# The even layer's gated and convolution projections in pairs of feature tiles by seven block products, with the context tiles beside the attention

## The chip, the cores and the metric

One core of a Trainium2 chip runs the whole program in one launch. The metric is device time in microseconds (us), the median over several executions. TensorE (PE) multiplies, VectorE (DVE), ScalarE (ACT) and GpSimd (POOL) do the rest, SyncE (SP) issues most of the DMAs.

## What is computed

A block of two layers on 1024 latent tokens (a grid of rows of 64) and 256 context tokens of width 1024, in float32. The even layer, cut to its core:

```
p = h @ w_in
q, k, v, g_a, a_f, a_b, c_b, c_c, c_x, g_b = _split_cols(p, EVEN_SIZES)
o_f, s_f = _gla_direction(q, k, v, log_gate(a_f, 0), s0_f)
o_b, s_b = _gla_direction(fl(q), fl(k), fl(v), fl(log_gate(a_b, 1)), s0_b)
o = _rmsnorm(o_f + fl(o_b), gla_g).reshape(bsz, length, GLA_V) * jax.nn.silu(g_a)
zc = _conv3_centered(c_c * c_x, conv_w)
y = c_b * zc * jax.nn.silu(g_b)
return jnp.concatenate([o, y], axis=-1), s_f, s_b
```

`_gla_direction` is a gated linear attention of 4 heads in chunks, forward and backward over the tokens. The odd layer is a recurrent unit in two directions. Each layer ends in an output projection, and the block in a norm.

## The kernel before

Features lie on the 128 partitions, tokens along the row. The normed input `h` of the even layer stays on chip as two float32r tensors, a high and a low part (`hhi`, `hlo`: 8 feature blocks by 1280 tokens). A product in float32 accuracy is three matmuls, `mm3`: high by high, high by low, low by high. A *unit* is one projection onto 128 features: `load_unit` loads its weights in two halves of 128x512 into the tiles `raw` (two buffers for the whole kernel) and `load_split` splits each by a ScalarE cast (line 111) and a VectorE subtraction (line 112) into a tile `hl` (six buffers). `proj` then multiplies it by the token chunks `CH`, 256 context tokens and twice 512 latents: 8 x 3 = 24 matmuls a chunk.

The gates of the attention (`emit_raw_gate`, units `w0f[8..15]`), and for each of eight feature tiles the convolution's four units (`emit_conv`: `cc`, `cx`, `cb` and its gate, `w0f[16..47]`) are 40 units in all. Their results go to DRAM (`gt_d`, `y0_d`). `presplit` splits the odd layer's weights in advance into DRAM (`w1s_d`), 20 halves a head, through the same `raw` and `hl` tiles.

The attention `emit_gla` runs a head at a time: three chunks backward, then three forward. A chunk is a gate (`pz`, a matmul, then ScalarE and VectorE in turn and a scan), factors (`qh`, `kh`, `k1`), transposes (`pk`), scores (`psc`), states (`pst`) and, forward, outputs (`po`), all in three PSUM banks of tag `G`, given out in program order. A scheduler orders each engine's instructions at build time: the program gives the priority, and what comes later fills in where what comes first is not ready. Behind head h the program has two gates, one convolution tile and 20 presplits, then q, k and v of the next head:

```
            for h in range(H):
                emit_gla(h)
                emit_raw_gate(w0f[8 + 2 * h], 2 * h)
                presplit(5)
...
                if h + 1 < H:
                    emit_qk(h + 1)
                    emit_v(h + 1)
    for ct in range(H, KD - 1):
        run(emit_conv(ct))
    run(emit_conv(KD - 1, CH[:2]))
```

Then come the remaining convolution tiles, under which the odd layer's modulation (`mod`, VectorE reductions `junk` of 128x1024 weights `wt`, line 586) runs, and the output projection (`out_group`), whose operands `ga` and `y` are loaded from `gt_d`, `oT_d` and `y0_d`. The last tile's last chunk is kept for between its groups (`rest`).

Of the kernel before, what the change touches and what calls it, by code (L numbers as in the profile page):

```python
# [28 lines left out]
H = 4  # L29
# [16 lines left out]
def hybrid_kernel(ctx: ExitStack, tc, xin, crow, frow, cols, consts, masks, w0f, w0va, w0v, wa2, wmT,  # L46
# [68 lines left out]
    def load_unit(src, name):  # L115
# [13 lines left out]
    hhi = hpool.tile([P, KD, T], F32R, name="hhi")  # L129
    hlo = hpool.tile([P, KD, T], F32R, name="hlo")  # L130

    def hk(k, c0, n):
        return hhi[:, k, c0:c0 + n], hlo[:, k, c0:c0 + n]

    def put_h(f, c0, n, ps, layer, sel, pool):

# [22 lines left out]

    w1s_d = dram.tile([5 * NB, P, 2, 512], F32, name="w1s_d")
    todo = [(b, j) for b in range(NB) for j in range(5)]

# [21 lines left out]
            ws += [(hi[:, k * P:(k + 1) * P], lo[:, k * P:(k + 1) * P]) for k in range(4)]  # L186
        return ws

    def emit_raw_gate(src, i, chunks=CH, tag="A"):
        for ps, c0, n in proj(load_unit(src, f"gt{i}_{chunks[0][0]}"), f"gt{i}", chunks, tag):  # L190
# [4 lines left out]
    def emit_conv(ct, chunks=CH, tag="A"):  # L195


        t0, t1 = chunks[0][0], chunks[-1][0] + chunks[-1][1]
        nm = f"{ct}_{t0}"
        z = vp.tile([P, T], F32, tag="z", name=f"z{nm}")  # L200
        zc = vp.tile([P, T], F32, tag="zc", name=f"zc{nm}")
        for ps, c0, n in proj(load_unit(w0f[16 + 4 * ct], f"cc{nm}"), f"cc{ct}", chunks, tag):
            S.copy(z[:, c0:c0 + n], ps)
        for ps, c0, n in proj(load_unit(w0f[17 + 4 * ct], f"cx{nm}"), f"cx{ct}", chunks, tag):
            V.tensor_tensor(z[:, c0:c0 + n], ps, z[:, c0:c0 + n], ALU.mult)
        V.tensor_scalar(zc[:, t0:t1], z[:, t0:t1], C("cw", 8 + ct), None, op0=ALU.mult)
        for lo_, hi_, w in ((t0, min(t1, NCTX), NCTX), (max(t0, NCTX), t1, 64)):
            if hi_ <= lo_:
                continue
            zr = z[:, lo_:hi_].rearrange("p (r i) -> p r i", i=w)  # L210
            cr = zc[:, lo_:hi_].rearrange("p (r i) -> p r i", i=w)
            V.scalar_tensor_tensor(cr[:, :, 1:w], zr[:, :, 0:w - 1], C("cw", ct), cr[:, :, 1:w],
                                   op0=ALU.mult, op1=ALU.add)
            V.scalar_tensor_tensor(cr[:, :, 0:w - 1], zr[:, :, 1:w], C("cw", 16 + ct), cr[:, :, 0:w - 1],
                                   op0=ALU.mult, op1=ALU.add)
        yield
        for ps, c0, n in proj(load_unit(w0f[18 + 4 * ct], f"cb{nm}"), f"cb{ct}", chunks, tag):
            V.tensor_tensor(zc[:, c0:c0 + n], ps, zc[:, c0:c0 + n], ALU.mult)  # L218
        SY.dma_start(y0_d[ct, :, t0:t1], zc[:, t0:t1])
        yield  # L220
        emit_raw_gate(w0f[19 + 4 * ct], 8 + ct, chunks, tag)

    def run(steps):
        for _ in steps:
            pass

    with sbuf("att") as ap:
# [124 lines left out]
        with sbuf("gla") as gp:  # L352
# [216 lines left out]
    for ct in range(H, KD - 1):  # L569
        run(emit_conv(ct))  # L570
    run(emit_conv(KD - 1, CH[:2]))

    rest = emit_conv(KD - 1, CH[2:], "B")


    with sbuf("mod") as mp:
# [36 lines left out]
        V.scalar_tensor_tensor(pl, pl, 2.0, mx, op0=ALU.mult, op1=ALU.add)  # L613
        V.tensor_scalar(rsc, pl, -8.0, None, op0=ALU.mult)
        V.tensor_scalar(rsh, pl, 4.0, None, op0=ALU.mult)

    def bcast_row(pool, ones, layer, s, name, tag):

# [447 lines left out]
```

## Time and profile before

| | |
|---|---|
| median of 3 runs | 1989.78 us (1987.29 to 1997.84) |
| profiled execution | 2002.68 us, span 2000.9 us |
| PE busy | 1932.0 us (97%) |
| DVE, ACT, POOL busy | 1317.8 us (66%), 961.3 us (48%), 105.2 us (5%) |
| DMA | 311.45 MB, mean 156 GB/s |
| attention, first gate of a head to that of the next | 174.7, 177.2 and 178.1 us |

A busy share is the time in which an engine has an instruction in work, over the span. Idle time of an engine counts only where another waits for it. Matmuls overlap in their pipeline, so a matmul's price is the distance between starts, not its duration.

### The profile page before, as it was taken

What the parts mean: (1) busy time and instruction counts of PE and PEld (TensorE: products, weight loads), DVE (VectorE), ACT (ScalarE), POOL (GpSimd) and SP (SyncE); (2) the same over time, 40 slices, a digit from 0 to 9 for tenths busy, and PEclk for the clock granted to TensorE, in tenths of its full rate; (3) what the DMA queues carried; (4) which work ended last, traced back from release to release, by engine and by line L of the source; (5) the groups of instructions that cost most, each with busy time, mean ns of one, the idle gap of its engine ahead of it and who ended that gap; (6) DMA issues with size and microseconds to landing.
All of it is one profiled execution on the core that took longest, in us unless ns stands there. A gap on an engine that the chain in (4) does not pass through costs nothing.

```text
span 2000.9 us, 27096 instructions
## 1 busy us (share of the span) xinstructions
PE 1932.0 (97%) x9884; PEld 1588.5 (79%) x9884; DVE 1317.8 (66%) x2103; ACT 961.3 (48%) x1690; POOL 105.2 (5%) x154
## 2 busy tenths in 40 slices
PE   9899999999999999999999899999999999998988
PEld 5777898888788888888776678878888888876767
DVE  6746436543552554388557474689999999996595
ACT  4333344334433433311345444267777776876452
POOL 1000000000000000000000000201111010100000
PEclk9999999999999999999999999999999999999999
DMA  9256217514721751366655665434333343324782
GB/s 357 82 195 199 78 50 252 175 43 146 244 89 33 245 192 53 124 223 197 205 175 178 209 222 173 139 111 127 120 118 120 115 121 121 116 81 156 264 290 88
DMA packets 162522, 311.45 MB, mean 156 GB/s; under 512 B 16338, under 2 KB 37202, under 8 KB 162260
## 3 DMA queue, kind: packets, MB, share of 16 engines
q1 hardware_dynamic: 140628, 267.78, 40.1%
q0 software_dynamic: 21760, 41.95, 7.5%
q8 instruction: 77, 1.26, 0.3%
q14 instruction: 57, 0.47, 0.1%
HBM read 221.05 MB, written 88.60 MB: 155 GB/s over the span
## 4 chain that ended last, share of the span: by engine, by line
PE 60%; DMA 19%; DVE 12%; ACT 5%; issue 4%; SPq 1%; POOL 0%; DVEq 0%; ACTq 0%; POOLq 0%
PE pjgt L126 4%; PE pjgt L127 4%; PE pjgt L125 4%; DMA rawpre<-in_w1f 4%; PE pjxr L125 4%; PE pjxr L127 4%; PE pjxr L126 4%; PE pO L126 3%; PE pO L125 3%; PE pO L127 3%; PE po L515 2%; DMA wt<-in_wmT 2%; DMA rawo<-in_w0out 2%; PE pv L125 2%; PE pv L126 2%
## 5 line engine op out<-in xcount | busy, mean ns | idle before, releaser
L125 PE MATMUL pjgt<-hhi,wgt 128*128 128x512 f32 (+1 forms) x640 | 240.6, 376 | 6.0 <-DVE zc L218 6.0
L125 PE MATMUL pO<-wo,yh 128*128 128x512 f32 x576 | 224.2, 405 | 17.6 <-ACT wo L111 16.6
L126 PE MATMUL pjgt<-hlo,wgt 128*128 128x512 f32 (+1 forms) x640 | 240.5, 376 | 0.0
L127 PE MATMUL pjgt<-hhi,wgt 128*128 128x512 f32 (+1 forms) x640 | 239.5, 376 | 0.0
L126 PE MATMUL pO<-wo,yh 128*128 128x512 f32 x576 | 231.1, 402 | 7.2 <-DVE wo L112 7.2
L127 PE MATMUL pO<-wo,yl 128*128 128x512 f32 x576 | 228.5, 399 | 0.0
L806 DVE SCALAR_TENSOR_TENSOR xc<-xp,col,xc 128x1283 f32<-128x1283 f32 (+2 forms) x102 | 149.8, 1476 | 3.2
L111 ACT CAST wo<-rawo 128x512 fp32r<-128x512 f32 x160 | 98.0, 619 | 110.7 <-DMA rawo<-in_w0out 74.9
L112 DVE TENSOR_TENSOR wo<-rawo,wo 128x512 fp32r<-128x512 f32 x160 | 108.5, 687 | 63.6 <-ACT wo L111 63.0
L125 PEld LDWEIGHTS pO<-wo,yh 128*128 128x128 f32 x576 | 109.3, 191 | 50.0 <-ACT wo L111 22.5
L125 PEld LDWEIGHTS pjgt<-hhi,wgt 128*128 128x128 f32 x640 | 121.0, 189 | 30.1 <-DVE zc L218 6.6
L126 PEld LDWEIGHTS pjgt<-hlo,wgt 128*128 128x128 f32 x640 | 121.1, 189 | 23.7 <-issue 1.1
L127 PEld LDWEIGHTS pjgt<-hhi,wgt 128*128 128x128 f32 x640 | 120.5, 189 | 23.4 <-issue 0.7
L126 PEld LDWEIGHTS pO<-wo,yh 128*128 128x128 f32 x576 | 109.7, 190 | 36.8 <-DVE wo L112 12.4
L125 PE MATMUL pjxr<-hhi,wxr 128*128 128x512 f32 (+1 forms) x384 | 137.4, 359 | 0.0
L126 PE MATMUL pjxr<-hlo,wxr 128*128 128x512 f32 (+1 forms) x384 | 137.1, 358 | 0.0
L127 PE MATMUL pjxr<-hhi,wxr 128*128 128x512 f32 (+1 forms) x384 | 136.8, 358 | 0.0
L127 PEld LDWEIGHTS pO<-wo,yl 128*128 128x128 f32 x576 | 109.8, 191 | 24.6 <-DVE yl L685 0.3
L112 DVE TENSOR_TENSOR wpre<-rawpre,wpre 128x512 fp32r<-128x512 f32 x80 | 55.1, 690 | 90.1 <-ACT wpre L111 89.7
L125 PE MATMUL pv<-wv,hhi 128*128 128x256 f32 (+1 forms) x320 | 91.8, 287 | 2.4 <-ACT v L387 2.4
L127 PE MATMUL pv<-wv,hlo 128*128 128x256 f32 (+1 forms) x320 | 92.9, 290 | 0.0
L126 PE MATMUL pv<-wv,hhi 128*128 128x256 f32 (+1 forms) x320 | 92.8, 290 | 0.0
(270 smaller groups left out, 4527.9 us busy)
## 6 DMA issues: line engine op xcount, KB each, us to landing
w1s_d<-wpre SPq DMA_DIRECT2D x160, 256.0 KB, 2.6
rawo<-in_w0out SPq DMA_DIRECT2D x96, 256.0 KB, 3.2
rawpre<-in_w1f SPq DMA_DIRECT2D x64, 256.0 KB, 3.1
wt<-in_wmT SPq DMA_DIRECT2D x32, 512.0 KB, 4.3
rawo<-in_w1out SPq DMA_DIRECT2D x64, 256.0 KB, 3.3
wxr<-w1s_d POOLq DMA_DIRECT2D x32, 512.0 KB, 3.8
wgt<-w1s_d POOLq DMA_DIRECT2D x32, 512.0 KB, 3.8
wm<-in_wmT SPq DMA_DIRECT2D x24, 512.0 KB, 8.1
```

What stands on the lines that cost most here:

```text
L111: S.copy(hi, raw)
L112: V.tensor_tensor(lo, raw, hi.bitcast(F32), ALU.subtract)
L125: PE.matmul(ps, a[0], b[0], start=first, stop=False)
L126: PE.matmul(ps, a[0], b[1], start=False, stop=False)
L127: PE.matmul(ps, a[1], b[0], start=False, stop=last)
L515: PE.matmul(ps[:, :DV], l, r, start=(i == 0), stop=(i == len(pairs) - 1))
L806: V.scalar_tensor_tensor(x, tap(j), cw[j], x, op0=ALU.mult, op1=ALU.add)
```

## The change

The latents' part of 36 units (eight gates, and the convolution's tiles without the last one, paired 0 with 4, 1 with 5, 2 with 6, and tile 3's four units in two pairs) moves behind the attention and is computed in 18 pairs. A pair of units times the latents is a 2x2 block product: two units by two halves of the input features, times two halves of the features by two halves of the tokens. It is done by seven block products instead of eight (Winograd's form of Strassen's): `pair` forms four combinations of raw weights on VectorE and splits them, `make_t` forms four combinations of `h` once and splits them into `T2`, `T3` and over parts of `hL` and `hC`, which are free by then (one quarter is put aside in DRAM, `b12_d`, and loaded back). Each product is 12 matmuls of 512 columns.

The context's part of the same units stays beside the attention, ten units of 256 tokens a head. Since `pair` needs three of each pair's four weight halves in split form, the context units also store theirs (`w0s_d`, two stores of 256 KB a half, 108 in all). `h` is now four tensors, high and low of the context (`hC`) and of the latents (`hL`). Of the last tile the context and first latent chunk stay as before.

```
--- before.py
+++ after.py
+            if i < len(save) and save[i] is not None:
+                for j, part in enumerate((hi, lo)):
+                    SY.dma_start(save[i][:, j], part.bitcast(F32))
...
             for h in range(H):
                 emit_gla(h)
-                emit_raw_gate(w0f[8 + 2 * h], 2 * h)
-                presplit(5)
-                emit_raw_gate(w0f[9 + 2 * h], 2 * h + 1)
-                presplit(5)
-                for _ in emit_conv(h):
+                for i in (2 * h, 2 * h + 1):
+                    emit_raw_gate(8 + i, i, CH[:1])
+                    presplit(5)
+                    run(emit_conv(i, CH[0]))
                     presplit(5)
...
+        for k in range(4):
...
+            b11, b12, b22, b21 = raw(k, 256), raw(k, 768), raw(4 + k, 768), raw(4 + k, 256)
+            V.tensor_tensor(b11, b12, b11, ALU.subtract)
+            V.tensor_tensor(b12, b22, b12, ALU.subtract)
+            V.tensor_tensor(b22, b22, b11, ALU.subtract)
+            V.tensor_tensor(b21, b21, b22, ALU.subtract)
+            for j, r, dst in ((1, b11, [t[:, k, 512:] for t in hL]), (2, b22, [t[:, k] for t in t23[0]]),
+                              (3, b12, [t[:, k] for t in t23[1]]), (4, b21, [t[:, k] for t in hv])):
+                S.copy(dst[0], r)
+                V.tensor_tensor(dst[1], r, dst[0].bitcast(F32), ALU.subtract)
...
+        x1, u2, u4, u5 = (tp.tile([P, 512], F32, tag=f"u{i}", bufs=1, name=f"u{i}{nm}") for i in range(4))
+        a11 = saved(0, 0)
+        r11, r21, r22, r12 = raw(0, 0), raw(1, 0), raw(1, 1), raw(0, 1)
+        p = product("A", a11, block(0, 256))
+        S.copy(x1, p)
+        V.tensor_tensor(r21, r11, r21, ALU.subtract)
+        V.tensor_tensor(r22, r22, r21, ALU.subtract)
+        s2 = parts(r22, "s2")
+        a12 = saved(0, 1)
+        p = product("A", s2, comb(2))
+        V.tensor_tensor(u2, p, x1, ALU.add)
+        V.tensor_tensor(r11, r22, r11, ALU.add)
+        s1 = parts(r11, "s1")
+        put(0, 0, product("G", a12, block(4, 256)), x1, x1)
+        s3 = parts(r21, "s3")
+        p5 = product("G", s1, comb(1))
+        V.tensor_tensor(u4, p5, u2, ALU.add)
+        a22 = saved(1, 1)
+        V.tensor_tensor(u2, product("A", s3, comb(3)), u2, ALU.add)
+        put(1, 1, p5, u2, u5)
+        V.tensor_tensor(r12, r12, r22, ALU.subtract)
+        s4 = parts(r12, "s4")
+        put(1, 0, product("A", a22, comb(4)), u2, u2)
+        put(0, 1, product("G", s4, block(4, 768)), u4, u4)
...
-    for ct in range(H, KD - 1):
-        run(emit_conv(ct))
-    run(emit_conv(KD - 1, CH[:2]))
...
+    T_ = make_t(tp)
+    for _ in emit_conv(KD - 1, CH[1]):
+        pass
...
+    for units, nm, put, around in jobs:
...
+        pair(tp, T_, units, nm, put)
...
+    for i in range(2):
+        G.dma_start(hL[i][:, 0:4, 512:], b12_d[i])
```

The built program of the change has 9089 rows of PE where the one before has 9305. Between the second and the third backward gate of head 1 (`pz1_1_768` and `pz1_1_256`), 45 matmuls of 256 and 62 of 512 columns of projections stand on PE before, and 60 of 256 in the change. SP's queue of the change, beside the attention of head 1 (`raw...` are loads of weights, `w0s_d` the new stores, `w1s_d` those of `presplit`):

```order
L189 DMA w1s_d_97<-wpre4_4_3456 128x512 x2
L97 DMA rawcc2_0_1_3470<-in_w0f 128x512
L122 DMA w0s_d_95<-wcc2_0_0_3465 128x512 x2
L97 DMA rawcx2_0_0_3503<-in_w0f 128x512
L122 DMA w0s_d_95<-wcc2_0_1_3472 128x512 x2
L97 DMA rawcx2_0_1_3510<-in_w0f 128x512
L122 DMA w0s_d_95<-wcx2_0_0_3505 128x512 x2
L97 DMA rawcb2_0_0_3546<-in_w0f 128x512
```

Before, the loads of a convolution unit had no store of their own weights between them; now each load stands behind the stores of the half before it.

VectorE of the change at the end of the attention (`rvo3_9` belongs to the last output of head 3, lines 599 to 610 are `make_t`, `junk0` and `modc` the modulation, `l_` small tiles of its end):

```order
L88 TENSOR_SCALAR rvo3_9_6555<-sso3_9_6553 128x1
L599 TENSOR_TENSOR b0_256_7111<-hL0_86,hL1_87 128x512
L599 TENSOR_TENSOR b0_768_7113<-hL0_86,hL1_87 128x512
L599 TENSOR_TENSOR b4_768_7115<-hL0_86,hL1_87 128x512
L599 TENSOR_TENSOR b4_256_7117<-hL0_86,hL1_87 128x512
...
L755 ISA junk0_9855,modc_9852<-wt0_9853,crb_9849 128x1024
L755 ISA modc_9852 128x1
L610 TENSOR_TENSOR T3_1_7108<-b0_768_7113,T3_0_7107 128x512
...
L665 TENSOR_TENSOR rga001_7355<-rga001_7355,rga011_7353 128x512
L630 TENSOR_TENSOR sga0s2_7373<-rga011_7353,sga0s2_7373 128x512
```

From the row behind `rvo3_9` to `sga0s2` are 113 rows; before, the reductions `junk` stood among the projections of tiles 4 to 7. PE of the change at the same place (`po3_9` and `pot3_9` are the last output and its transposes, `pga0` the first pair's products, the first by `hL`, the second by `T2` and `sga0s2`):

```order
L532 MATMUL po3_9_6548<-S0_3_8_6546,qf3_768_6435 128x256
L130 MATMUL pga0_7357<-hL0_86,aga000_7347 128x512
...
L130 MATMUL pga0_7357<-hL0_86,aga000_7347 128x512
L539 MATMUL pot3_9_6560<-ident_72,on3_9_6552 128x128 x2
L128 MATMUL pga0_7378<-T2_0_7105,sga0s2_7373 128x512
L129 MATMUL pga0_7378<-T2_1_7106,sga0s2_7373 128x512
```

Ten matmuls of the first product stand between the last output and the second product; before, twelve units of the tiles 4 to 6 and most of tile 7 stood behind the last head.

## Rows read from the trace of the kernel before

**Rows 1.** The page, parts 1 and 2: TensorE's busy time and granted clock.

```profile
PE 1932.0 (97%) x9884; PEld 1588.5 (79%) x9884; DVE 1317.8 (66%) x2103; ACT 961.3 (48%) x1690; POOL 105.2 (5%) x154
...
PEclk9999999999999999999999999999999999999999
```

**Rows 2.** Windows: length, then busy us (instructions) by engine, PEclk, DMA share, GB/s.

```profile
296.00:376.00 80.00, 79.69 (x436) 65.32 (x434) 48.82 (x100) 36.54 (x82) 0.00 (x0) 1.00 0.73 243
376.00:474.00 98.00, 96.83 (x609) 85.04 (x608) 35.93 (x84) 36.92 (x97) 5.47 (x10) 1.00 0.19 57
```

**Rows 3.** Timeline of PE, projections (start us, us): 24 starts of each width.

```profile
955.73 0.40 PE L125 MATMUL pjcx<-hhi,wcx 128*128 128x512 f32 x1
...
961.09 0.40 PE L127 MATMUL pjcx<-hhi,wcx 128*128 128x512 f32 x1
961.33 0.28 PE L125 MATMUL pjcb<-hhi,wcb 128*128 128x256 f32 x1
...
964.05 0.28 PE L127 MATMUL pjcb<-hhi,wcb 128*128 128x256 f32 x1
```

**Rows 4.** Timeline of PE: the first gate matmul of heads 1, 2 and 3.

```profile
298.00 0.38 PE L411 MATMUL pz<-aT,wst 64*128 64x256 f32 x1
...
475.21 0.38 PE L411 MATMUL pz<-aT,wst 64*128 64x256 f32 x1
...
653.26 0.38 PE L411 MATMUL pz<-aT,wst 64*128 64x256 f32 x1
```

**Rows 5.** Timeline of PE behind a wait ([idle before <-releaser]).

```profile
977.08 0.79 PE L125 MATMUL pjgt<-hhi,wgt 128*128 128x512 f32 x1 [4.32 <-DVE zc L218]
977.67 0.63 PE L126 MATMUL pjgt<-hlo,wgt 128*128 128x512 f32 x1
...
981.94 0.63 PE L127 MATMUL pjgt<-hhi,wgt 128*128 128x512 f32 x1
```

**Rows 6.** Timeline of ACT and DVE: first and last instruction of two chunks' factors.

```profile
298.41 0.47 ACT L414 ACTIVATE b<-pz,col 128x256 f32<-128x256 f32 x1
...
304.44 0.29 DVE L457 TENSOR_TENSOR k<-k,k 128x128 f32<-128x128 f32 x1
...
316.40 0.70 ACT L414 ACTIVATE b<-pz,col 128x512 f32<-128x512 f32 x1
...
326.50 0.42 DVE L458 TENSOR_TENSOR k<-kh,ends 128x256 f32<-128x256 f32 x1
```

**Rows 7.** Lines: count | busy us, mean ns of one | idle before, releaser.

```profile
L509 DVE SCALAR_TENSOR_TENSOR S<-S,dec,pst 128x256 f32<-128x256 f32 x64 | 30.6, 478 | 8.0 <-PE pst L504 5.9 <-DVE rvo L88 0.3 <-PE pz L411 0.3
...
L90 POOL TENSOR_TENSOR rro<-rvo,m 128x1 f32<-128x1 f32 x40 | 21.9, 548 | 741.9 <-DVE rvo L88 741.9
...
L519 ACT ACTIVATE on<-po,rro 128x256 f32<-128x256 f32 x40 | 18.9, 473 | 14.3 <-POOL rro L90 13.8
...
L466 ACT COPY k1T<-pk 128x512 f32<-128x512 f32 (+1 forms) x24 | 12.3, 511 | 17.3 <-PE pk L465 17.2
```

**Rows 8.** Windows of line 112 alone: length, DVE busy (instructions), PEclk, DMA.

```profile
296.00:376.00 80.00, 20.69 (x30) 1.00 0.73 243
```

**Rows 9.** Timeline of DVE: two instructions of 128x512 in a row.

```profile
324.02 0.68 DVE L459 TENSOR_TENSOR qh<-qh,q 128x512 f32<-128x512 f32 x1
324.63 0.68 DVE L456 TENSOR_TENSOR kh<-kh,k 128x512 f32<-128x512 f32 x1
```

**Rows 10.** Timeline of DVE: the modulation's reductions.

```profile
879.24 1.23 DVE L586 CUSTOM_DVE_ANT_0 junk<-wt,crb 128x1024 bf16<-128x1024 f32 x1 [1.90 <-DMA wt<-in_wmT]
...
880.50 1.23 DVE L586 CUSTOM_DVE_ANT_0 junk<-wt,crb 128x1024 bf16<-128x1024 f32 x1
```

**Rows 11.** Lines: SiLU and cast of the output projection's operands.

```profile
L668 ACT ACTIVATE ga<-ga 128x512 f32<-128x512 f32 (+1 forms) x80 | 46.9, 588 | 87.3 <-DMA ga<-gt_d 65.2 <-DMA ga<-g_d 20.4 <-DVE wo L112 1.4
...
L684 ACT CAST yh<-y 128x512 fp32r<-128x512 f32 (+1 forms) x80 | 45.8, 574 | 48.1 <-DVE y L681 21.8 <-PE pO L126 20.3 <-DVE y L679 5.7
```

**Rows 12.** DMA issues: count, KB each, median us to landing.

```profile
ga<-gt_d SPq DMA_DIRECT2D x32, 192.0 KB, 2.9
```

More of the change, by code (lines that the diff above doesn't have):

```diff
@@ L113, in load_split, with load_unit @@
         return hi, lo
-    def load_unit(src, name):
+    def load_unit(src, name, save=()):
         ws = []
@@ L193, in emit_raw_gate @@
             SY.dma_start(gt_d[i, :, c0:c0 + n], s[:, :n])
[L195 to L215, printed above, removed]
@@ new lines, in emit_conv @@
+    def emit_conv(ct, chunk, tag="A"):
+        c0, n = chunk
+        nm = f"{ct}_{c0}"
+        z = vp.tile([P, 512], F32, tag="z", name=f"z{nm}")[:, :n]
+        zc = vp.tile([P, 512], F32, tag="zc", name=f"zc{nm}")[:, :n]
+        for ps, _, _ in proj(load_unit(w0f[16 + 4 * ct], f"cc{nm}", kept(16 + 4 * ct, c0)), f"cc{ct}", [chunk], tag):
+            S.copy(z, ps)
+        for ps, _, _ in proj(load_unit(w0f[17 + 4 * ct], f"cx{nm}", kept(17 + 4 * ct, c0)), f"cx{ct}", [chunk], tag):
+            V.tensor_tensor(z, ps, z, ALU.mult)
+        short_conv(ct, zc, z, NCTX if c0 == 0 else 64)
@@ L568, in hybrid_kernel, with make_t, raw @@
                     emit_v(h + 1)
-    for ct in range(H, KD - 1):
-        run(emit_conv(ct))
-    run(emit_conv(KD - 1, CH[:2]))
-    rest = emit_conv(KD - 1, CH[2:], "B")
+    def make_t(tp):
+        t23 = [[tp.tile([P, 4, 512], F32R, name=f"T{j}_{i}") for i in range(2)] for j in (2, 3)]
+        for i in range(2):
+            SY.dma_start(b12_d[i], hL[i][:, 0:4, 512:].bitcast(F32))
+        hv = [t.rearrange("p (k a) n -> p k (a n)", a=2) for t in hC]
+        T = {}
+        for k in range(4):
+            def raw(kk, c0):
+                r = tp.tile([P, 512], F32, tag="r", bufs=4, name=f"b{kk}_{c0}")
+                hi, lo = hk(kk, c0, 512)
+                V.tensor_tensor(r, hi.bitcast(F32), lo.bitcast(F32), ALU.add)
+                return r
+            b11, b12, b22, b21 = raw(k, 256), raw(k, 768), raw(4 + k, 768), raw(4 + k, 256)
[7 more added lines that the diff above has]
+                V.tensor_tensor(dst[1], r, dst[0].bitcast(F32), ALU.subtract)
+                T[j, k] = tuple(dst)
+        return T
@@ new lines, in pair, with raw, saved, parts @@
+    def pair(tp, T, units, nm, put):
+        def raw(i, half):
+            r = tp.tile([P, 512], F32, tag="r", bufs=4, name=f"r{nm}{i}{half}")
+            load(r, w0f[units[i]][:, 512 * half:512 * half + 512])
+            return r
+        def saved(i, half):
+            hl = wpool.tile([P, 2, UW], F32R, tag="hl", bufs=6, name=f"a{nm}{i}{half}")[:, :, :512]
+            G.dma_start(hl, w0s_d[units[i], half])
+            return hl[:, 0], hl[:, 1]
+        def parts(r, name):
+            hl = wpool.tile([P, 2, UW], F32R, tag="hl", bufs=6, name=f"s{nm}{name}")
+            hi, lo = hl[:, 0, :512], hl[:, 1, :512]
+            S.copy(hi, r)
+            V.tensor_tensor(lo, r, hi.bitcast(F32), ALU.subtract)
+            return hi, lo
+        def product(tag, a, b):
+            ps = bank(tag, f"p{nm}")
+            for k in range(4):
+                mm3(ps, [t[:, k * P:(k + 1) * P] for t in a], b[k], k == 0, k == 3)
+            return ps
+        def block(k0, c0):
+            return [hk(k0 + k, c0, 512) for k in range(4)]
+        def comb(j):
+            return [T[j, k] for k in range(4)]
+        x1, u2, u4, u5 = (tp.tile([P, 512], F32, tag=f"u{i}", bufs=1, name=f"u{i}{nm}") for i in range(4))
[22 more added lines that the diff above has]
+        put(0, 1, product("G", s4, block(4, 768)), u4, u4)
@@ new lines, in hybrid_kernel, with start, conv @@
+    jobs = []
+    for i in range(0, 8, 2):
+        jobs.append(((8 + i, 9 + i), f"ga{i}", lambda r, *a, i=i: put_gate0(i + r, *a), None))
+    for ct in range(3):
+        c = (ct, ct + 4)
+        def start(c=c):
+            for i in c:
+                zt(zs, i)
+        def conv(c=c):
+            for i in c:
+                short_conv(i, zt(zcs, i), zs[i], 64)
+        fs = [lambda r, *a, c=c: put_z(c[r], *a), lambda r, *a, c=c: put_mul(zs[c[r]], *a),
+              lambda r, *a, c=c: put_y(c[r], *a), lambda r, *a, c=c: put_gate0(8 + c[r], *a)]
+        for j, nm in enumerate(("cc", "cx", "cb", "gb")):
+            o = 16 + j
+            jobs.append(((o + 4 * c[0], o + 4 * c[1]), f"{nm}{ct}", fs[j],
+                         (start, None) if j == 0 else (None, conv) if j == 1 else None))
@@ new lines, in hybrid_kernel @@
+    jobs.append(((28, 29), "cc3", put_ab, (lambda: zt(zs, 3), lambda: short_conv(3, zt(zcs, 3), zs[3], 64))))
+    jobs.append(((30, 31), "cb3", lambda r, *a: put_gate0(11, *a) if r else put_y(3, *a), None))
+    for units, nm, put, around in jobs:
+        before, after = around or (None, None)
+        if before:
+            before()
+        pair(tp, T_, units, nm, put)
+        if after:
+            after()
+    for i in range(2):
+        G.dma_start(hL[i][:, 0:4, 512:], b12_d[i])
+    rest = emit_conv(KD - 1, CH[2], "B")
@@ L615, in hybrid_kernel @@
         V.tensor_scalar(rsh, pl, 4.0, None, op0=ALU.mult)
+    tp_scope.close()
     def bcast_row(pool, ones, layer, s, name, tag):
```

60 lines of the change are left out of this document (51 added, 9 removed).

## Prediction

> **What bounds the kernel now.** I read the page first: TensorE (PE) is busy 97% of the span and the granted clock stands at its upper level in all slices [rows 1]. A mean hides stages, so the windows come next. In the attention two stretches alternate for each head. In the first, 296 to 376 us, PE is busy 79.69 of 80 us, VectorE 48.82, ScalarE 36.54 and the DMA engines 0.73; in the second the DMA share is 0.19 and PE is still full [rows 2]. The reader should see that nothing but PE is full there, and that PE is full because projections of the latents lie between the steps of the attention.
>
> The PE timeline gives the pace: in 24 matmuls of 512 columns the starts are (961.09 - 955.73)/23 = 0.233 us apart, in 24 of 256 columns (964.05 - 961.33)/23 = 0.118 us [rows 3]. The gate matmul that opens a head starts at 298.00, 475.21 and 653.26 us: 177.2 and 178.1 us a head, mean 177.6 [rows 4]. Six units of the cover (24 matmuls of 256 and 48 of 512 columns each, 14.0 us) take 84, the next head's q and k two units, 28, its v 240 matmuls of 256 columns, 28. So 37 us are the attention's own matmuls.
>
> **The change, part by part.** *Matmuls that go.* A pair of units on the latents took 2 x 2 x 24 = 96 matmuls of 512 columns; seven products of 12 are 84. Eighteen pairs save 216, at 0.233 us 50.3 us. The wait at 972 us, 4.32 us for `zc` and then 12 matmuls 0.427 apart ((981.94 - 977.67)/10) where 0.233 is the pace [rows 5], goes too, because that unit is no longer alone: 4.3 + 12 x 0.194 = 6.6 us.
>
> *The attention loses its cover.* The latents' halves of the 24 units that lay beside it move behind it; ten context units a head stay, 240 matmuls of 256 columns, 28 us. By the built order the PE work between a head's first gate and its last output is 37 + 28 + some 6 us of the next q: 72 us. How long does the attention need by itself? Gate, scan and factors of a chunk run from ScalarE's first instruction to VectorE's last: 298.41 to 304.73, 6.3 us for the context chunk, 316.40 to 326.92, 10.5 us for 512 columns, with weight splits among them [rows 6]. A head does this for three chunks in two directions: 2 x 27.3 = 55 us. The next chunk's gate can't be far ahead, since gate, scores, states and outputs take the three `G` banks in turn. Behind the factors a backward chunk has the transposes, their copy (0.51 us), a state matmul and two updates (0.48 each) before a bank is free: about 3 us. A forward chunk has the masks and, for every two tiles, a square, the power on GpSimd (0.55), the scaling (0.47) and a state update [rows 7]: about 5 us for the context chunk, 10 for the next and 15 with the last outputs. 55 + 9 + 30 gives 94 us, an estimate and the lower end.
>
> The upper end is the two `raw` buffers. From 296 to 376 us VectorE split 30 weight halves, one in 2.67 us [rows 8]. After the change 44 of them stand between the first gate and the last output of a head (20 of `presplit`, 20 of context units, 8 for the next head, less the four ahead of the gate), on the same in-order queues as the attention: 117 us. The new saves share SP's queue and the DMA engines: heads 0 and 1 move 126 and 122 transfers of 256 KB and some 2 MB of outputs, 35 and 34 MB, and at the 243 GB/s of that stretch [rows 2] 44/48 of it need about 130 us. I take 105 us, between 94 and 117, since both limits hold at once and neither alone. PE then waits 105 - 72 = 33 us in heads 0 to 2; in head 3, where the last unit's first latent chunk adds 83 matmuls of 512 columns, 105 - 85 = 20. Together +119 us (94: 75; 117: 167; with 130 in heads 0 and 1: 193).
>
> What do these waits do to the clock? After the one wait of 4.32 us the next matmuls ran at the lower level, 1.2 GHz, and lost 2.3 us [rows 5]. In the attention I charge nothing for that, since PE has slack there. The Trainium skill ("TensorE: Matmul & The Clock Gate", section "HAM oscillation — how this bites in real kernels") says that a kernel whose matmul groups are short beside the waits between them starts cold again in group after group, and the one restart in this trace agrees. By that rule PE would run the whole attention at half pace and the sum would be +310 us where mine is +128; it is the third rival below.
>
> *The combinations of the latents.* By the order `make_t` stands on VectorE behind the last `rvo3_9`, and PE has ten matmuls of the first product left then. The next product needs `s2`, 113 VectorE instructions on: 48 of `make_t` and 5 of the pair, each 128x512; 17 of the modulation's 1024-wide reductions, which before lay under projections; the rest tiny. At 0.61 us from start to start [rows 9] and 1.26 [rows 10], 53 x 0.61 + 17 x 1.26 + 26 x about 0.1 = 56 us, less 2 of PE's rest: 54 us of idle PE, and 2.3 us for the restart at the lower clock [rows 5]. Bounds 50 (some instructions overlap more) and 62 (the reductions wait for `wt`).
>
> *The first operands of the output projection.* SP's order has the loads `ga0_0_0` and `y0_0_0` behind the last pair's stores, so behind PE's last product: two vector instructions (0.61 each), a load of 2.9 us [rows 12], the SiLU (0.59), a multiply, the cast (0.57) [rows 11] and a subtraction, about 8 us, plus 2.3 for the restart: 10 us (4 to 16).
>
> *Costed at nothing.* In the pairs VectorE has 15 to 19 instructions of 128x512, 9 to 12 us, in 84 x 0.233 = 19.6 us of PE; two convolutions after `cx` fill one more pair nearly, and without that cover it would be 3 us in three places. A pair's 2.6 MB are 134 GB/s, below what rows 2 carry. The context matmuls were 256 wide before. The load that puts `hL` back has group 0 of the output projection above it.
>
> Sum: -50.3 - 6.6 + 119 + 56 + 10 = +128 us. The profiled run took 2002.68 us, 12.9 over the median of 1989.78 us; from the median, 2118 us.
>
> **The rivals.** *The attention stays covered*: its chain needs no more than PE's 72 us, so the 119 us vanish, and 1989.8 - 57 + 66 = 1999 us, 0.5% over; with hole and first operands at their lower ends (54) 1987, no change. For it: the scheduler put context units between all steps. Against: between two backward gates of head 1 stood 45 matmuls of 256 and 62 of 512 columns, 20 us, now 60 of 256, 7 us, where factors and states take 13. It decides from a chain of 72 us a head. To be faster by over 0.5% the hole would have to shrink as well, and VectorE's order excludes most of that.
>
> *The load ring binds by bytes*: about 130 us in the first two heads and more than 117 in the others, 2200 us and a little over. For it: 108 new stores of 256 KB. Against: the DMA share is 0.73 and not 1 where the ring ran before [rows 2], so the wait is partly latency, which more bytes don't lengthen.
>
> *Half clock through the attention*: 2 x 72 = 144 us in heads 0 to 2 and 170 in head 3, instead of 105, +182: 2300 us. For it: rows 5. Against: v and k run dense for some 45 us in each head, and PE's waits there should mostly be shorter than that one.
>
> **How the numbers follow.** The forecast, the sum with 94 to 130 us a head, 0.76: from -57 + 75 + 50 + 6 = +74 to -57 + 193 + 62 + 16 = +214, 2064 to 2204 us. Attention partly covered, 2000 to 2064 us, 0.08. Wholly covered, 1980 to 2000 us, 0.04; faster, 0.03. Above 2204 us, by bytes or by the clock, 0.09. The range 2055 to 2210 us holds about 8 in 10. About 0.5% (10 us) is what this kernel's runs can tell from no change: faster 0.03, same 0.04, slower 0.93.
>
> **What would show it.** Right: PE busy about 70% between a head's first gate and last output, gates of successive heads some 155 us apart, one PE gap near 54 us after the last `po`, and pairs 19.6 us apart. Wrong: PE full in the attention (then the chain is shorter than I add it up), a gap well under 50 us after it, or a pair that takes more than 22 us.

## The result, and the profile after

The changed kernel takes 2212.3 us in the median of 4 runs (2209.5 to 2215.8), the kernel before 1992.3 us on the same chip (1987.3 to 1997.8): 1.110 times as long, 95% interval 1.107 to 1.114. The forecast was 2118 us in a range up to 2210.

The page of the profiled execution (span 2210.8 us), TensorE's busy time and granted clock, as [rows 1]:

```profile
PE 1954.3 (88%) x9668; PEld 1593.8 (72%) x9668; DVE 1525.6 (69%) x2437; ACT 999.3 (45%) x1760; POOL 145.6 (7%) x210
...
PEclk9988987897897959999999999999999999999999
```

TensorE is busy for longer than before with 216 fewer matmuls, and no slice of 40 after the 15th shows a lowered clock (a digit under 9). So the first place to look is before 15/40 x 2211 = 829 us. Timeline of PE: the first gate matmul of each head, as [rows 4], the gates of the last two forward chunks of head 1, and the last output of heads 0, 1 and 3:

```profile
117.27 0.38 PE L428 MATMUL pz<-aT,wst 64*128 64x256 f32 x1 [1.01 <-DVE aT L415]
...
256.50 0.59 PE L532 MATMUL po<-S,qf 128*128 128x256 f32 x2
...
291.53 0.38 PE L428 MATMUL pz<-aT,wst 64*128 64x256 f32 x1
...
352.43 0.50 PE L428 MATMUL pz<-aT,wst 64*128 64x512 f32 x1
...
385.98 0.50 PE L428 MATMUL pz<-aT,wst 64*128 64x512 f32 x1
...
416.39 0.59 PE L532 MATMUL po<-S,qf 128*128 128x256 f32 x2
...
467.77 0.38 PE L428 MATMUL pz<-aT,wst 64*128 64x256 f32 x1
...
640.42 0.39 PE L428 MATMUL pz<-aT,wst 64*128 64x256 f32 x1
...
773.91 0.59 PE L532 MATMUL po<-S,qf 128*128 128x256 f32 x2
```

The heads come 174.3, 176.2 and 172.6 us apart. Before it was 177.6, with 288 matmuls of 512 columns more (67 us) and 96 of 256 fewer (11 us) in every head. These 56 us went behind the attention, and the heads came hardly closer; only head 3, behind which no further head stands, ended earlier (134 us behind its first gate instead of 180). Windows from gate to gate, then from the first gate to the end of the last output of heads 0, 1 and 3 (columns as in [rows 2]):

```profile
117.27:291.53 174.26, 134.59 (x819) 114.93 (x819) 86.37 (x189) 72.04 (x175) 5.48 (x10) 0.86 0.58 195
291.53:467.77 176.24, 140.93 (x844) 120.82 (x843) 86.68 (x190) 72.74 (x178) 5.65 (x10) 0.83 0.58 194
467.77:640.42 172.65, 134.89 (x844) 116.78 (x843) 85.63 (x190) 73.12 (x178) 5.47 (x10) 0.86 0.53 180
...
117.27:257.09 139.82, 100.15 (x549) 81.87 (x550) 83.50 (x184) 63.66 (x155) 4.93 (x9) 0.83 0.67 228
291.53:416.98 125.45, 90.14 (x492) 74.06 (x492) 81.73 (x182) 60.75 (x151) 5.10 (x9) 0.76 0.73 248
...
640.42:774.50 134.08, 102.13 (x554) 82.27 (x554) 86.44 (x190) 63.24 (x156) 5.80 (x10) 0.82 0.62 207
```

No engine is full there: TensorE waits 35 to 40 us a head and is stretched by a granted clock of 0.83 to 0.86 (part of the time at 1.2 GHz instead of 2.4), VectorE and the DMA engines have room. This points to a chain of steps that wait for each other. The longest wait of TensorE in head 1, then the longest of ACT (us in total, times, longest; first gate to last output):

```profile
PE psc L501 <- DVE kh L473: 17.4, 3, 6.5
...
ACT wpre L111 <- DMA rawpre<-in_w1f: 10.4, 11, 2.4
ACT k1T L483 <- PE pk L482: 7.4, 5, 3.2
ACT wcc L111 <- DMA rawcc<-in_w0f: 5.9, 4, 2.6
ACT wcb L111 <- DMA rawcb<-in_w0f: 5.9, 3, 2.8
ACT wpre L111 <- DMA rawpre<-in_w1ax: 4.9, 3, 3.5
```

TensorE waits most for `kh`, one of a chunk's factors: the attention's own chain. ACT, which works in that chain, waits for weights. Added up over all `raw` tiles of the head from gate to gate it is 41.4 us in which ACT stood before a cast whose weights had not landed. In the kernel before, the same sum is 34.8 us: the waits were there already, beside a TensorE that was full. One place where such a wait holds up a step of the attention is in ACT's timeline at the end of that head:

```profile
403.71 0.20 ACT L535 ACTIVATION_READ_ACCUMULATOR on<-po 128x1 f32 x1
406.95 0.62 ACT L111 CAST wq<-rawq 128x512 fp32r<-128x512 f32 x1 [3.05 <-DMA rawq<-in_w0f]
407.48 0.47 ACT L536 ACTIVATE on<-po,rro 128x256 f32<-128x256 f32 x1
```

The scaling of an output at 407.48 stands in order behind a cast of the next head's `wq`, and that waited 3.05 us for its load; the power that the scaling needs had been done at 404.8, and the transposes on TensorE wait for the scaling.

Behind the attention, timeline of PE at the combinations of the latents:

```profile
776.88 0.38 PE L539 MATMUL pot<-ident,on 128*128 128x128 f32 x2
831.80 0.80 PE L128 MATMUL pga<-T,sga0s 128*128 128x512 f32 x1 [54.53 <-ACT sga0s L629]
...
834.32 0.80 PE L128 MATMUL pga<-T,sga0s 128*128 128x512 f32 x1 [1.30 <-ACT sga0s L629]
...
839.60 0.59 PE L128 MATMUL pga<-hL,aga 128*128 128x512 f32 x1
```

A gap of 54.53 us, then a product of 12 matmuls in 7.8 us, 5.0 more than 12 x 0.233. A window of the pairs, and the start of the output projection on PE, whose last matmul of the pairs began at 1186.30:

```profile
860.00:880.00 20.00, 20.00 (x88) 16.09 (x87) 17.98 (x35) 2.97 (x5) 2.26 (x4) 1.00 0.93 284
```

```profile
1191.27 2.06 PE L797 MATMUL pggate<-dggate,ones 128*128 128x128 f32 x8 [4.57 <-DVE dggate L796]
1196.80 1.22 PE L797 MATMUL pggate<-dggate,ones 128*128 128x128 f32 x4 [3.47 <-DVE dggate L796]
1197.84 0.80 PE L128 MATMUL pO<-wo,yh 128*128 128x512 f32 x1
```

The pairs are dense at the upper clock level, though the DMA engines are busy 0.93 of the time in this window; the output projection loses some 10 us.

### The profile page after: what moved, and what is told of

It reads as the page before. It is cut to its first block, busy times and chain, and to the rows that moved or that the text cites. A ratio compares the mean times of both kernels' runs of the same rounds, so it can differ in the third digit from the quotient of the medians.

```text
span 2210.8 us, 27773 instructions
## 1 busy us (share of the span) xinstructions
PE 1954.3 (88%) x9668; PEld 1593.8 (72%) x9668; DVE 1525.6 (69%) x2437; ACT 999.3 (45%) x1760; POOL 145.6 (7%) x210
## 3 DMA queue, kind: packets, MB, share of 16 engines
q0 software_dynamic: 37504, 72.36, 11.3%
## 5 line engine op out<-in xcount | busy, mean ns | idle before, releaser
L130 PE MATMUL pjgt<-hL,wgt 128*128 128x512 f32 x272 | 107.7, 396 | 0.5 <-DVE wgt L112 0.5
L128 PE MATMUL pjgt<-hL,wgt 128*128 128x512 f32 x272 | 107.5, 395 | 0.0
L129 PE MATMUL pjgt<-hL,wgt 128*128 128x512 f32 x272 | 107.5, 395 | 0.0
L128 PE MATMUL pjxr<-hL,wxr 128*128 128x512 f32 x256 | 101.5, 397 | 0.0
L129 PE MATMUL pjxr<-hL,wxr 128*128 128x512 f32 x256 | 101.0, 396 | 0.0
L130 PE MATMUL pjxr<-hL,wxr 128*128 128x512 f32 x256 | 100.8, 395 | 0.0
L111 ACT CAST wpre<-rawpre 128x512 fp32r<-128x512 f32 x80 | 49.3, 616 | 68.1 <-DMA rawpre<-in_w1f 51.3
L839 ACT ACTIVATE ga<-ga 128x512 f32<-128x512 f32 (+1 forms) x80 | 46.9, 588 | 71.2 <-DMA ga<-gt_d 49.8
L1075 DVE TENSOR_TENSOR_SCAN a<-a,i 128x1024 f32<-128x1024 f32 x32 | 75.3, 2352 | 1.1
L129 PE MATMUL pv<-wv,hL 128*128 128x256 f32 (+1 forms) x256 | 72.9, 285 | 0.0
L130 PE MATMUL pv<-wv,hL 128*128 128x256 f32 (+1 forms) x256 | 72.6, 284 | 0.0
L128 PE MATMUL pv<-wv,hL 128*128 128x256 f32 (+1 forms) x256 | 72.6, 283 | 0.0
```

What stands on the lines that cost most here:

```text
L128: PE.matmul(ps, a[0], b[0], start=first, stop=False)
L839: silu = S.activation(ga, ga, AF.Silu)
L1075: V.tensor_tensor_scan(rv[3], rv[4], rv[5], rv[0][:, 255:256], op0=ALU.mult, op1=ALU.add)
```

## The experiments

Twelve kernels ran, eight of them beside single runs of the kernel before (1993.6 and 1994.5 us), four beside 7 runs (median 1994.9); all but e8 ran once, so differences under 10 us are not read. "Heads" are the distances of the first gate matmuls of heads 0 to 3; "attention" runs from the first of them to the end of head 3's last output; both were read from each run's timeline of PE.

```
kernel                          time     heads                 attention
before                          1992.3   174.7 177.2 178.1     709.7
the change                      2212.3   174.3 176.2 172.6     657.2
e1  no saves                    2187.3   170.8 169.9 164.5     638.4
e2  four raw                    2142.5   151.3 153.3 153.9     587.0
e3  presplit later              2187.8   138.4 132.4 138.0     530.7
e4  warm                        2224.0   174.7 178.1 173.9     666.6
e5  e1 + e3                     2184.1   132.4 139.2 136.6     525.3
e6  gates back                  2149.1   167.4 175.2 174.2     662.5
e7  direct products, no saves   2179.3   165.9 170.2 163.7     634.0
e8  hybrid                      2057.2   173.4 178.6 178.9     699.0
e9  reductions held             2198.7   172.0 176.0 174.6     656.8
e10 e1 + e2 + e9                2107.3   147.7 148.6 147.4     570.5
e11 warm, gates alone           2208.9   169.3 174.3 175.4     656.7
e12 presplit on GpSimd          2235.6   123.1 181.5 183.9     677.7
```

**Less load on the ring: e1, e2, e3.** The ring is the row of `raw` buffers through which weight halves come in; A is the time from a head's first gate to the end of its last output. The first edit is e1's (`saved` then loads and splits the half itself), the second e2's (`more_raw` is the attention's pool), the last two are e3's.

```diff
     def kept(u, c0):
-        if c0 or u >= 44:
...
+        return ()
...
+        if more_raw and next(raws) % 2:
+            raw = more_raw[0].tile([P, 512], F32, tag="raw", bufs=2, name=f"raw{name}")[:, :n]
...
                     emit_raw_gate(8 + i, i, CH[:1])
-                    presplit(5)
                     run(emit_conv(i, CH[0]))
-                    presplit(5)
...
         pair(tp, T_, units, nm, put)
+        presplit(5)
```

> The 108 stores of split weights are gone; the pairs load these halves whole and split them themselves (same arithmetic). A is the time from a head's first gate to its last output, 125, 131 and 133 us in heads 1 to 3 of the change. Theory 'load ring': the weight halves come one after another through SP's queue, where a load stands behind the stores of the half before it, and ACT and DVE wait in order for them; without the stores a half takes 2.67 us or less again, A falls to 117 us or below, and the time to about 2150 us (2130 to 2175). Theory 'clock': A is long because TensorE falls to 1.2 GHz again and again (granted 0.75 to 0.82 there); stores don't matter, A stays within 4 us and the time within 2195 to 2225. Theory 'chain': the attention's own steps need 125 us, the same 2195 to 2225.

> Four buffers for weight halves that come in instead of two, in the attention alone. Load ring, if it is the time from issue to landing that limits: A falls from 125 to 133 us to 110 or less, time 2110 to 2160 us. Load ring, if the bytes or the order of SP's queue limit: A within 5 us, time 2190 to 2220. Clock and chain: no change either, 2195 to 2225 us.

> The 80 weight halves that are split in advance for the second layer move from the attention to the pairs (five behind each of the first 16 pairs), so 24 of 44 halves a head stay beside the attention; TensorE's work there is unchanged. Load ring: A falls by about 20 x 1.5 to 20 x 2.7 us until the chain binds, to some 95 to 105 us, and the time by 4 x 25 to 4 x 35 to 2070 to 2115 us, if the pairs (19.6 us of TensorE each) take the splits for nothing. Clock or chain: A within 5 us and the time 2195 to 2225 us, more if the pairs are slowed.

e2 is the clear one: 2142.5 us, 70 less than the change, and its attention is 70.2 us shorter. Nothing but two more buffers for arriving halves was added; the program, its bytes and its stores stayed. Its ACT waits for `raw` tiles in head 1 are 8.7 us instead of 41.4. That A would fall to 110 didn't hold: A is 128 to 135 us. With the loads earlier the scheduler draws all of the next head's q and k and 58 to 78 of the 240 matmuls of its v in front of the last output, where the change has 36 to 118 of q and k and none of v. So A no longer measures heads 0 to 2, and the distance of the gates does: from a head's last output to the next gate it is 19 to 22 us instead of 34 to 51. In head 3, behind which no q, k or v stands, A fell by 5.6 us only (128.5). So most of the 70 us is work of the next head that now fills waits; no run separates that from loads which merely land earlier. Head 1 of e2, gate to gate, then heads 1 and 2 of e3 and A of its head 3:

```profile
269.94:423.23 153.29, 129.61 (x843) 114.10 (x843) 85.19 (x190) 72.59 (x179) 5.47 (x10) 0.91 0.64 223
```

```profile
258.06:390.44 132.38, 123.88 (x841) 108.44 (x840) 73.71 (x170) 61.70 (x157) 5.49 (x10) 1.00 0.42 138
390.44:528.44 138.00, 123.91 (x846) 109.89 (x845) 73.24 (x170) 62.39 (x159) 5.50 (x10) 0.98 0.34 112
...
528.44:650.37 121.93, 96.91 (x563) 79.22 (x562) 73.57 (x170) 53.62 (x136) 5.82 (x10) 0.90 0.30 101
```

With more bytes in the same time (223 against 194 GB/s) e2's head is shorter, so bytes didn't bind. In e3, with 24 halves a head instead of 44, TensorE is busy 124 of 132 to 138 us in heads 1 and 2 and stays near the upper level (granted 0.98 and 1.00): 8 to 14 us of waits are left where the next head's q, k and v fill in. In head 3, where they can't, 25 us of waits are left and A is still 121.9 us. e1 gave 25 us, two fifths of what its theory wanted, and ACT's waits for `raw` tiles in its head 1 are 41.9 us, no less than in the change: the new stores are a small part of it.

But e3's time fell by 24 us, though its attention is 126 us shorter. The other hundred went to the pairs, where the splits now stand. Waits of SP's queue in e3 from 740 to 1140 us:

```profile
SPq L189 <- ACT wpre L111: 78.5, 49, 4.8
SPq L189 <- DVE wpre L112: 54.2, 46, 4.6
...
PE pga L128 <- DMA aga<-w0s_d: 19.0, 3, 9.1
```

The stores of the splits wait for ACT and VectorE on SP's queue, and the loads behind them wait too. The last line is one of TensorE's own waits from 700 to 1140 us: 55 us in all for halves that were saved split (`aga<-w0s_d` and the like), and these are issued by GpSimd, not behind SP's stores, at a DMA share of 0.71 to 1.02 from 720 us on. So e3 alone doesn't tell order from bytes.

**Bytes or order in the pairs: e5.** The edits of e1 and e3 together.

> The stores of split weights are gone (pairs split all their halves themselves) and the 80 splits for the second layer stand behind the first 16 pairs. Where only the latter was moved, the heads came 132 to 138 us apart and the last output of head 3 ended 124 us earlier, but the pairs, at 6.4 MB each, took 24 us and more at a DMA share of 0.9 to 1.0 and gave 100 us back. Theory 'bytes in the pairs': at 1.8 MB for the pair and 3.8 MB for five splits, 5.6 MB in 19.6 us are 287 GB/s, below the 320 to 358 GB/s that those windows moved; the pairs take 20 to 21 us again and the time is 2075 to 2110 us. Theory 'order': the loads of the pair stand behind the splits' stores on SP's queue and VectorE has 24 to 27 instructions of 0.61 us a pair beside the reductions; the pairs stay at 23 us and more, time 2130 to 2190 us. In either case the heads stay 130 to 138 us apart (load ring); a clock or chain theory for the attention would have them return to 155 or more.

2184.1 us, in the range of the order theory. PE's waits from 700 to 1140 us, and one window:

```profile
PE pga L128 <- ACT sga0s L622: 52.2, 1, 52.2
PE pga L128 <- ACT waga L111: 27.3, 3, 10.6
PE pcc L128 <- ACT wacc L111: 23.8, 4, 9.5
...
800.00:820.00 20.00, 13.31 (x58) 10.37 (x56) 16.21 (x28) 3.10 (x5) 0.00 (x0) 0.89 0.98 363
```

From 820 to 1120 us the DMA share is 0.58 to 0.87 in its windows of 20 us with TensorE busy 15 to 20 of them, while the change itself ran its pairs dense at 0.93: there bytes don't bind. From 720 to 820 us the share is 0.93 to 0.98 with TensorE busy 9 to 19 of 20, and bytes aren't excluded. What binds behind 820 us is not separated either: e5 also moved the loads of the saved halves to SP's queue and gave ACT and VectorE their splits.

**The clock: e4, e11.** Both have the first edit, e4 alone the second; nothing of the computation is left out.

```diff
-                p3 = bank("G", f"psc{h}_{d}_{t0}").rearrange("p (t i) -> p t i", i=P)
+                p3 = bank("G", f"psc{h}_{d}_{t0}")
+                for _ in range(12):
+                    PE.matmul(p3, rmask[:, :P], rmask, start=True, stop=True)
+                p3 = p3.rearrange("p (t i) -> p t i", i=P)
...
                 ps = bank("G", f"pst{h}_{d}_{t}")
+                for _ in range(4):
+                    PE.matmul(ps[:, DV:], rmask[:, :P], rmask[:, :DV], start=True, stop=True)
```

> Extra matmuls whose results nobody reads are added to the attention (12 of 512 columns behind each gate matmul, 4 of 256 beside each state matmul, some 23 us a head at the upper clock level), in banks that are taken anyway. Clock: the granted clock between a head's first gate and last output rises from 0.75 to 0.82 to above 0.9, A falls by 10 to 20 us a head although TensorE does more, time 2130 to 2175 us. Load ring: the clock rises as well, but A stays within 4 us, 2200 to 2225. Chain with TensorE on it: A grows by up to 15 us a head, 2225 to 2275 us.

> Again matmuls whose results nobody reads, now only 12 of 512 columns behind each gate matmul (15 us a head), where the factors are computed and no step of the attention waits for TensorE, and none beside the state matmuls, where they stood in the chain. Clock: granted clock above 0.88 between a head's gate and last output and heads 160 to 168 us apart instead of 172.6 to 176, time 2165 to 2195 us. Load ring: the clock rises the same, the heads stay 172 to 178 us apart, time 2203 to 2222 us.

Windows of e11 from gate to gate:

```profile
116.88:286.14 169.26, 143.36 (x890) 118.30 (x891) 86.44 (x189) 70.95 (x175) 5.48 (x10) 0.92 0.59 200
286.14:460.46 174.32, 145.92 (x915) 120.08 (x915) 86.90 (x190) 72.58 (x178) 5.48 (x10) 0.93 0.58 197
460.46:635.87 175.41, 152.61 (x916) 126.43 (x915) 85.97 (x190) 72.95 (x178) 5.47 (x10) 0.88 0.53 177
```

The granted clock rises from 0.83 to 0.86 to 0.88 to 0.93 and the time stays (2208.9). In e4 the clock between a head's first gate and last output was 0.91 to 0.94 and the time 2224.0, 12 us more than the change; its second kind of matmul stands in the chain of the states, which may be why. A grew in two of three heads by more than the 4 us that the ring theory allowed. The theory that the clock lengthens the attention gets no support: the slow matmuls seem to lie where TensorE would wait. It isn't a clean test, since the added matmuls themselves take 16.8 us a head (72 x 0.233); e6 is the second one.

**Is TensorE's slack real: e6.**

```diff
-                    emit_raw_gate(8 + i, i, CH[:1])
+                    emit_raw_gate(8 + i, i)
...
-    for i in range(0, 8, 2):
-        jobs.append(((8 + i, 9 + i), f"ga{i}", lambda r, *a, i=i: put_gate0(i + r, *a), None))
```

> The eight gate units do their latents beside the attention again, by direct products (2 x 48 matmuls of 512 columns, 22.4 us of TensorE a head), and the four pairs of gate units are gone (4 x 19.6 = 78 us) with 12 of their stores. Load ring: the 174 us a head are set by the weight halves, of which there are as many as before, so the matmuls go into TensorE's 35 us of waits and the time that it runs at the lower clock: 172 to 180 us a head, time 2120 to 2150 us. If TensorE is itself on the path of the attention through its clock or its order: up to 22 us more a head, 2190 to 2225 us.

2149.1 us, 63 less: 78 us of pairs went, and 22 us of TensorE's work more in each head cost next to nothing (heads 167 to 175 us apart, the attention 5 us longer), at a granted clock of 0.93 to 0.94. By the theory that TensorE is on the path it would have been 2190 and more.

**The products themselves: e7.** `make_t` is gone and each pair does `proj` of its two units on `CH[1:]`, the rest as e1.

> The order of the change without its seven products: each pair's two units are done by direct products on the latents (96 matmuls of 512 columns), there are no combinations of the latents, and no stores of split weights. Beside the kernel with seven products and no stores (2187 us): +50 us for 216 matmuls at 0.233 us, -56 us for the stretch in which TensorE waits for the combinations, 2170 to 2190 us. If TensorE's wait behind the attention is mostly the reductions of the modulation, which stay, it would be +50 - 35 = 2195 to 2205 us.

2179.3 us against e1's 2187.3: without the products it is 8 us less, as the 50.3 us for 216 matmuls against the gap and its restart would have it. Two single runs tell no more than that the products gain nothing here.

**The gap behind the attention: e9.** The modulation's loads go by `load`, with `not_before[0]` set to the last load of the second pair.

> The modulation's loads stand behind those of the second pair, so its reductions leave the stretch in which TensorE waits for the combinations of the latents: by the built order 77 rows of VectorE instead of 113 stand between the last power of the attention and the second product's operand, none of them a reduction. By the prediction's sum for that stretch (53 x 0.61 + 17 x 1.26 + small ones) it falls from 54 to 32 to 35 us, time 2188 to 2198 us. If the loads of the first pair or the copies on ACT set it, it stays above 45 us and the time above 2203. If the reductions cost the pairs or the output projection as much later: the gap falls, the time doesn't.

Timeline of PE in e9, the first product that needs combinations:

```profile
815.74 0.80 PE L128 MATMUL pga<-T,sga0s 128*128 128x512 f32 x1 [38.78 <-ACT sga0s L629]
```

38.78 us instead of 54.53, and 2198.7 us, 13.6 less: both a little short of what was expected. The reductions were 16 us of the gap (17 x 1.26 = 21 were counted), and nearly all of that came off the time. The rest are `make_t`'s own instructions; one of them waited 3.22 us for a cast on ACT.

**Order or rate of the ring: e12.** Does a half cost because ACT and VectorE stand in order before it, or because each buffer is held for so long? `presplit`'s cast and subtraction are done by GpSimd.

```diff
-        S.copy(hi, raw)
-        V.tensor_tensor(lo, raw, hi.bitcast(F32), ALU.subtract)
+        (eng.tensor_copy if eng else S.copy)(hi, raw)
+        (eng or V).tensor_tensor(lo, raw, hi.bitcast(F32), ALU.subtract)
```

> The 80 splits for the second layer are done by GpSimd (cast and subtraction) instead of ACT and VectorE; loads, buffers, stores and SP's queue are those of the change. Load ring as a matter of rate (44 halves a head through two buffers, each held from its load to its split): GpSimd isn't faster than ACT and VectorE, so the heads stay 172 us apart or get longer, time 2205 to 2300 us. Load ring as a matter of order (ACT and VectorE wait in order for a half to land, and the attention's next step stands behind that): 20 of 44 halves no longer stop them, heads 150 to 165 us apart, time 2130 to 2180 us, less what GpSimd's own wait does to the power of each output that it computes.

2235.6 us. Lines of GpSimd from 290 to 466 us:

```profile
L112 POOL TENSOR_TENSOR wpre<-rawpre,wpre 128x512 fp32r<-128x512 f32 x20 | 27.2, 1363 | 0.9
L111 POOL CAST wpre<-rawpre 128x512 fp32r<-128x512 f32 x20 | 13.3, 665 | 115.4 <-PE pv L130 57.0 <-DVE wgt L112 31.4 <-DMA rawpre<-in_w1f 19.6
```

Taking 20 of 44 halves off ACT and VectorE bought nothing: 2235.6 us, the attention 20 us longer, heads 1 and 2 some 182 and 184 us long though ACT's waits for `raw` tiles fell to 29.9 and 23.2 us in them. That is in the range of the reading as a rate, but doesn't show it. GpSimd's subtraction takes 1363 ns (690 on VectorE), so it holds the buffer for longer; but GpSimd also stood 57.0 us in one wait for the next head's v (`pv` in the second line), the scheduler drew the next head's gate ahead (head 0 has 123 us), and GpSimd's power for each output stands behind its splits.

**Put together: e10 and e8.** e10 is e1, e2 and e9 in one.

> Four buffers for halves that come in, no stores of split weights, and the reductions held back, together. Singly the first two gave 70 and 25 us. Load ring: both act on the same wait, so together less than their sum, 75 to 95 us, and 15 to 20 us for the reductions: 2097 to 2122 us; heads 146 to 152 us apart. If they act on different waits, 95 us and more: 2080 to 2097. In either case slower than the kernel before by over 4%, since the attention without its cover has periods above 122 us and the combinations still stand open.

2107.3 us, 105 less than the change: 14 us as in e9 and 91 for e1 and e2 together, which is in the range for a shared wait but too near their sum of 95 to tell it from separate ones. It is the best form with all 18 pairs that ran, 5.7% over the kernel before.

e8 goes back to the cover of the kernel before and uses products behind it only: five pairs, tiles 4 and 5 and the last two units of tile 6, whose first two are done directly ahead of `make_t`.

```diff
-                    emit_raw_gate(8 + i, i, CH[:1])
...
+                emit_raw_gate(8 + 2 * h, 2 * h)
+                presplit(5)
...
+    for ct in range(H, KD):
+        run(emit_conv(ct, CH[:1]))
+    run(emit_conv(KD - 1, CH[1:2]))
...
     T_ = make_t(tp)
```

> The attention keeps the cover of the kernel before (gates and tiles 0 to 3 on all 1280 columns, no stores of split weights). Behind it stand direct units that don't need the combinations: tile 7's first latents and two units of tile 6, 39 us of TensorE beside some 40 us of VectorE for the combinations; then five pairs by seven products (tiles 4, 5 and half of 6); the modulation's reductions begin behind the second pair's loads. Load ring (so no loss where TensorE's cover is long): heads 175 to 178 us apart as before, no gap over 5 us behind the last output, 5 x 12 matmuls x 0.233 = 14 us less and the 6.6 us wait gone: 1965 to 1985 us. If the reductions delay the output projection, or the combinations still show as a gap: 1990 to 2020 us.

2057.2 us, 1.031 times the kernel before (1.029 to 1.033), above both of the ranges that were expected. The attention did as expected, 699 us against 710 before. What it lost stands behind that; PE's waits from 820 to 1070 us, and one of VectorE's from 960 to 1060 us:

```profile
PE pggate L807 <- DVE dggate L806: 34.7, 1, 34.7
PE pO L128 <- ACT yh L865: 15.6, 1, 15.6
PE pcc L128 <- ACT scc4s L634: 14.8, 1, 14.8
...
DVE junk L765 <- DMA wt<-in_wmT: 12.5, 9, 2.4
```

65 us. The combinations still stick out by 14.8 us, and the reductions that were held back (`junk`) arrive on VectorE at the start of the output projection, whose gate rows (`dggate`) stand behind them. VectorE is full from 920 to 980 us; at the end of the stretch the last reductions wait for their own loads. In e9, where 18 pairs stand above the output projection, TensorE waits 7.8 us for the gate rows. A version that spreads the reductions over the output projection's first group wasn't tried; none of the kernels that ran beats the kernel before.

## Why the prediction was wrong, point by point

*Direction and mechanisms.* Slower, by the attention without its cover and by the gap behind it: both hold. The sum came to +128 us; the measured change is +220.

*The step that failed* is the size of the attention's term: "I take 105 us, between 94 and 117, since both limits hold at once and neither alone." A was 139.8, 125.5, 131.3 and 134.1 us (start of the first gate to the end of the last output), above both ends. By the distance of the gates it is 174 instead of 155 us, 58 us in three heads, and 29 in head 3 (134 - 105), 87 in all. That alone would have made the forecast 2205. Both limits were set too low:

- The upper end, from the ring. 2.67 us a half was measured beside a TensorE that was full [rows 2, 8]. The trace has 42 to 45 halves in A, about as counted, but they came one in 2.92 to 3.18 us.
- The lower end, from the chain. In e3's head 3, with 20 halves fewer and no next head behind it, A is 121.9 us and TensorE waits 25 us, where 94 and 94 - 85 = 9 were counted (e5: 117.2 and 20). In head 1 of the change the last two forward chunks took 33.6 and 31.0 us from gate to gate and to the last output; 20.5 and 25.5 were added up. In heads 1 and 2 of e3 the waits are 8 to 14 us, fewer than the 22 counted, since work of the next head fills them, which the sum didn't have.

So a value between two limits had no support: A lay above both. e2 shows how much of it hangs on the ring. Two more buffers bring the heads to 151 to 154 us, near the 155 of the forecast, 65 us in all; of the 29 us of head 3 they take 6, and 20 halves fewer take 12 (17 in e5). What the rest of head 3 is stays open: a chain that was added up too short, or one that is slowed by what stands beside it.

*The rival "load ring by bytes"* came near in time (2200 and a little over) by a reason that doesn't hold: e2 moves the same bytes faster, and e1, with 27 stores a head less, gives 25 us. The argument against it in the prediction, that at a DMA share of 0.73 the wait is partly latency, was right, and should have been carried into the price.

*The clock* was charged nothing "since PE has slack there". By the profile alone that looks wrong: in A TensorE waited 35 to 40 us in heads 0 to 2, near the 33 of the forecast, and was busy 90 to 100 us instead of 72, at a granted clock of 0.76 to 0.83. But e11 raised the clock and e6 added 22 us of matmuls a head, and neither moved a head by more than 7 us, which bears the prediction out; that the clock costs exactly nothing isn't shown. The Trainium skill ("TensorE: Matmul & The Clock Gate", section "HAM oscillation — how this bites in real kernels") describes restarts at the lower clock in matmul group after matmul group. The trace agrees that the clock falls again and again there; the prediction's sum by that rule, +310 us, didn't come about, as the clock wasn't low throughout (that would be 0.50).

*The matmuls that go, the gap, the first operands.* 54.53 us against 54; the restart behind it cost 5.0 us (1.3 of it a further wait) against 2.3; the output projection began 11.3 us behind the last pair, 3.3 of it `pggate` matmuls, and some 2 us of restart, together about 10, against 10. Pairs dense, 88 matmuls in 20 us, against 19.6 us for 84. e7 fits the balance of 50 against 56 and a restart.

*The vector work of the pairs and 2.6 MB a pair at nothing*: right for the change, at a DMA share up to 0.93; wrong as soon as splits for another layer are put there (e3, e5).

*What was to show it.* TensorE's busy share in A was to be about 70%. It was 71 to 72% in heads 0 to 2 and 76% in head 3, but by luck: more busy time, much of it at a lowered clock, in a longer A. The gap and the pairs came as written, the distance of the gates didn't.

*The sums.* The lower ends of the gap and of the first operands are added up to 54 us in one place and to 56 in another; that changes nothing.

## What to carry to other kernels

Work beside a chain of small steps isn't idle filling: it also hides the latencies of everything else in the same queues, so before taking it away, add up all waits in that stretch (here 34.8 us a head of ACT before weight casts) and not only those of the chain. Where two limits share in-order engines, a value between them isn't a safe estimate: here the result lay above both. Look at what decides how early the next stage's work can begin: two more buffers for weights gave 70 us here, and 64 us of it is the shorter stretch between a head's last output and the next head's gate. Moving the ring's loads to another stage (e3) moved the loss with them; four buffers and moved loads together were not tried.

## What the runs showed of the hardware that wasn't expected

TensorE spent 11 to 17 us a head more on the same matmuls at the lowered clock (135 to 141 us against 124 in e3), and no run shows that it cost time; raising the clock by matmuls without use gave nothing (2208.9 us). DMA engines 0.93 busy didn't slow a stream of pairs, while in e5, from 820 to 1120 us, the pairs waited for weights with the DMA engines only 0.58 to 0.87 busy. A 128x512 subtraction into float32r takes 1363 ns on GpSimd, twice VectorE's 690 [rows 8], and the cast 665 ns, near the 0.62 us of ACT's cast of `wq` above.
